# Attention score products over 128 rows, query loads per tile, and norm sums in groups of 128 tokens

## The chip, the cores and the metric

The kernel runs on one core of a Trainium2 chip. The time is the device time of one execution, in microseconds (us). The engines are named as in the profile: PE is TensorE (PEld its weight loads), DVE is VectorE, ACT is ScalarE, POOL is GpSimd, and SP is SyncE, which only issues DMAs. POOL and SP each execute their queue in order, DMA issues included.

## What is computed

One step of a backbone of two layers over 128 prompt tokens and 512 latent tokens (a grid of 8 x 64), model width 1024. A layer normalises its input, runs four mixers A to D side by side, merges them, and ends with a feed-forward part. The change touches the norm, the scores of B (differential attention, 4 heads of two 64-wide maps) and those of D (neighbourhood attention, 8 heads of width 64):

```python
def _rmsnorm(x, g):
    y = xf * lax.rsqrt(jnp.mean(xf * xf, axis=-1, keepdims=True) + EPS)
...
def _diff_attend(q, k, v, lam):            # B
    p = jax.nn.softmax(jnp.einsum('bhqmd,bhkmd->bhmqk', qi, k).astype(F32) * scale, axis=-1)
    pd = p[:, :, 0] - lam * p[:, :, 1]
    return jnp.einsum('bhqk,bhkd->bhqd', pd, v.astype(F32)).astype(q.dtype)
...
def _na_latent(q, k, v, ck, cv, rpb):      # D, latent queries; 16-column window as a mask
    s_lat = jnp.einsum('bhqd,bhkd->bhqk', qi, ki).astype(F32) * scale + bias
    s_ctx = jnp.einsum('bhqd,bhkd->bhqk', qi.astype(F32), ckf) * scale
    p = jax.nn.softmax(jnp.concatenate([s_ctx, s_lat], axis=-1), axis=-1)
```

Prompt queries read the prompt's own keys alone; latent queries read 256 cached context keys and the latent keys.

## The kernel before

**Exact products from two parts.** Every large product is made of float32r operands split into a high and a low part (`split`: ACT copies the high part, DVE subtracts). A weight tile is loaded by SP into a raw buffer (`load_w`; two raw buffers), ACT casts it to `whi`, DVE makes 608 columns of the rest `wlo` and POOL the last 416. `unit` (line 292) then issues three products of 320 columns for each of eight feature tiles: high by high, low by high, high by low, all over 128 rows. One weight tile so feeds 48 products. In the profile they are `pu`, the "stream" of the text; `ptk` are products of the same kind with 256 columns.

**Who sets the order.** `weave` writes the order of PE by hand. The mixers are chains (Python generators) with ranks; a chain yields the tiles that its next PE work waits for, a rough clock says when they are there, and until then steps of the projections, gates and merges (`fill`) are issued. That clock charges a score product by its columns alone. DVE, ACT, POOL and SP get their order from a scheduler with priorities, and tiles of one pool are handed out as they come free. The pool `sa` has 18 tiles of 128 x 512 (`NSA`), shared by all chains. B and D both wait for branch A to be done, and then run side by side, with the stream between their steps.

**Scores of B** (`mix_b`, `b_tile`). `prep_b` leaves each head's turned queries and keys in DRAM (`bqk`), as blocks of 64 rows: high 0, low 0, low 1, high 1. `mix_b` loads for a head, on POOL's queue (`QM`): `qd`, for each of two maps the high part of all 512 queries twice, one copy under the other (64 + 64 rows); `ql`, both maps' low parts (128 rows, one map in each half); and `Kd`, per map the keys' high part over their low part. `split_ctx` makes the same of the 256 context keys (`Kc`). For one query tile of 128 and one map, `latent` then issues, for 512 latent keys and again for 256 context keys, two products into one bank: `qd` over 128 rows gives high by (high + low), `ql` over 64 rows adds low by high. Maximum, exponent, sum, turning and the product with the values follow in `b_tile`. The prompt tile is one product of 64 rows in plain float32 for either map.

**Scores of D** (`mix_d`). The same with head pairs in place of maps: `qd`, `ql`, `kd`, `kc`, loaded by SP (`QD`) from `dqk`. Queries come in four blocks of 16 columns (128 queries); a block reads 256 context keys and a window of 8 x 24 or 8 x 32 latent keys (`WIN`), so eight products: two heads, two key pieces, high and low. Line 1426 yields what they wait for.

**Norm** (`rstd_half`; for the first input, `first`). Squares of 320 tokens are summed over features by products with one column of ones, 64 tokens at a time; a chain of small DVE instructions (`rsqrt`) makes the factor; DVE spreads it on a diagonal (`dg`, 64 rows of 320), and a product with ones over 64 rows, `prs`, copies it to all partitions.

## Time and profile before

| what | value |
|---|---|
| median of 3 runs | 3595.67 us (3592.9 to 3596.69) |
| profiled execution, span from first to last instruction | 3582.7 us |
| PE busy | 3465.2 us, 97% |
| weight loads (PEld) busy | 3312.7 us, 92% |
| DVE busy | 2366.4 us, 66% |
| ACT busy | 1430.6 us, 40% |
| POOL busy | 511.7 us, 14% |

The span is 13.0 us under the median; what lies around it (start and end of the execution) is in no row. Shares of busy time are averages over stages that differ. Ends of products on PE are modelled and overlap, so the distance from one start to the next is what tells the cost of a product. The mixers of layer 0 fill the time to some 1200 us, merging and feed-forward that to some 1850, and layer 1 follows the same way.

### The profile page before, as it was taken

The numbers are of one execution on the slowest core, as the hardware profiler recorded it, in microseconds if no ns is written. First come the engines' busy times: TensorE is split into PE (matmuls) and PEld (weight loads), VectorE is DVE, ScalarE is ACT, GpSimd is POOL, SyncE is SP. The second block draws the span as 40 slices with busy tenths as digits, with TensorE's granted clock in tenths as the row PEclk, the third lists the DMA queues.
The fourth block names the chain that finished last, engine by engine and source line by source line (L and its number), as shares of the span: only waits on it lengthen the run. The fifth ranks groups of instructions, "written<-read, shape, count | busy, mean of one in ns | idle before, by whom it ended". The sixth has DMA issues, their size and how long they took to land.

```text
span 3582.7 us, 63638 instructions
## 1 busy us (share of the span) xinstructions
PE 3465.2 (97%) x24036; PEld 3312.7 (92%) x24036; DVE 2366.4 (66%) x5487; ACT 1430.6 (40%) x3170; POOL 511.7 (14%) x536
## 2 busy tenths in 40 slices
PE   8999999899999999999999999998999999999998
PEld 5988999888989999999999999998888999999998
DVE  7689888865566478787456897776444546634445
ACT  5344545444343253222253454554444433522222
POOL 2221112311112100000002212223121121000000
PEclk9999999999999999999999999999999999999999
DMA  6443434854243254444234433356343134312222
GB/s 217 152 151 129 128 109 135 250 155 144 94 139 110 96 172 143 150 150 131 82 120 140 143 120 105 104 158 205 112 138 120 59 99 146 115 63 77 80 77 71
DMA packets 282826, 455.96 MB, mean 127 GB/s; under 512 B 46996, under 2 KB 175636, under 8 KB 282520
## 3 DMA queue, kind: packets, MB, share of 16 engines
q1 hardware_dynamic: 272472, 421.48, 36.9%
q0 software_dynamic: 10048, 30.42, 2.8%
q8 instruction: 190, 3.11, 0.4%
q14 instruction: 116, 0.95, 0.1%
HBM read 364.23 MB, written 87.56 MB: 126 GB/s over the span
## 4 chain that ended last, share of the span: by engine, by line
PE 72%; DVE 6%; DMA 4%; issue 3%; ACT 2%; POOL 0%; SPq 0%; DVEq 0%; ACTq 0%; POOLq 0%
PE pu L150 53%; PE ptk L150 2%; PE pbs L150 2%; PE pds L150 2%; PE pdv L150 2%; PE pbo L150 1%; PE pW L150 1%; PE pX L150 1%; PE pca L150 1%; PE pdt L156 1%; PE pT L150 1%; DMA wraw<-in_wd 1%; PE pkS L150 1%; DVE wlo L105 1%; DMA moT<-oT 0%
## 5 line engine op out<-in xcount | busy, mean ns | idle before, releaser
L150 PE MATMUL pu<-hh,whi 128*128 128x320 f32 (+1 forms) x3760 | 1199.9, 320 | 18.3 <-ACT stg L105 15.7
L150 PE MATMUL pu<-hl,whi 128*128 128x320 f32 (+1 forms) x3760 | 1168.0, 311 | 2.9 <-DVE hl L105 2.9
L150 PE MATMUL pu<-hh,wlo 128*128 128x320 f32 (+1 forms) x3760 | 1168.5, 311 | 0.0
L150 PEld LDWEIGHTS pu<-hh,whi 128*128 128x128 f32 (+1 forms) x3760 | 710.6, 189 | 29.5 <-ACT stg L105 16.4
L150 PEld LDWEIGHTS pu<-hl,whi 128*128 128x128 f32 (+1 forms) x3760 | 710.8, 189 | 4.7 <-DVE hl L105 3.1
L150 PEld LDWEIGHTS pu<-hh,wlo 128*128 128x128 f32 (+1 forms) x3760 | 709.0, 189 | 1.7
L105 ACT CAST whi<-wraw 128x1024 fp32r<-128x1024 f32 (+2 forms) x410 | 390.7, 953 | 680.8 <-PE pu L150 441.3
L105 POOL TENSOR_TENSOR wlo<-wraw,whi 128x416 fp32r<-128x416 f32 (+1 forms) x209 | 320.5, 1534 | 1886.3 <-ACT whi L105 1409.2
L105 DVE TENSOR_TENSOR wlo<-wraw,whi 128x608 fp32r<-128x608 f32 (+3 forms) x410 | 385.6, 940 | 282.6 <-ACT whi L105 274.0
L150 PE MATMUL pu<-fa,whi 128*128 128x320 f32 x1152 | 253.7, 309 | 0.2 <-DVE x L105 0.2
L150 PE MATMUL pu<-mo,whi 128*128 128x320 f32 x1024 | 235.4, 317 | 5.4 <-DVE mo L105 3.4
L105 DVE SCALAR_TENSOR_TENSOR x<-pu,gn,x 128x128 f32<-128x128 f32 (+1 forms) x336 | 136.5, 435 | 88.1 <-PE pu L150 86.2
L150 PEld LDWEIGHTS pu<-fa,whi 128*128 128x128 f32 x1152 | 192.7, 188 | 0.5 <-PE pu L150 0.5
L150 PE MATMUL ptk<-whi,hh 128*128 128x256 f32 x640 | 192.5, 301 | 0.0
L150 PE MATMUL ptk<-wlo,hh 128*128 128x256 f32 x640 | 182.6, 285 | 3.2 <-DVE wlo L105 3.2
L150 PE MATMUL ptk<-whi,hl 128*128 128x256 f32 x640 | 182.5, 285 | 0.0
L491 DVE CUSTOM_DVE_ANT_0 junk<-wa,cs,mod 128x256 bf16<-128x256 f32 (+1 forms) x288 | 172.2, 598 | 14.6 <-DMA wa<-in_wada 10.5
L150 PEld LDWEIGHTS pu<-mo,whi 128*128 128x128 f32 x1024 | 171.8, 190 | 9.8 <-DVE mo L105 4.9
L150 PE MATMUL pu<-fa,wlo 128*128 128x320 f32 x576 | 177.8, 309 | 0.0
L150 PE MATMUL pu<-mo,wlo 128*128 128x320 f32 x512 | 159.6, 312 | 0.0
L150 PEld LDWEIGHTS ptk<-wlo,hh 128*128 128x128 f32 x640 | 124.0, 194 | 3.4 <-DVE wlo L105 3.4
L150 PEld LDWEIGHTS ptk<-whi,hh 128*128 128x128 f32 x640 | 124.2, 194 | 0.0
(426 smaller groups left out, 6170.1 us busy)
## 6 DMA issues: line engine op xcount, KB each, us to landing
wraw<-in_win SPq DMA_DIRECT2D x151, 512.0 KB, 3.8
wa<-in_wada SPq DMA_DIRECT2D x116, 256.0 KB, 2.9
wraw<-in_wg SPq DMA_DIRECT2D x44, 512.0 KB, 3.6
wraw<-in_wu SPq DMA_DIRECT2D x44, 512.0 KB, 3.6
wraw<-in_wd SPq DMA_DIRECT2D x80, 256.0 KB, 2.6
p<-stg SPq DMA_DIRECT2D x112, 160.0 KB, 3.3
wa<-in_wada SPq DMA_DIRECT2D x128, 128.0 KB, 2.5
wraw<-in_wtok SPq DMA_DIRECT2D x32, 512.0 KB, 4.0
```

What stands on the lines that cost most here:

```text
L105: r = f(*args, **kw)
L150: r = self.nc.tensor.matmul(out, lhsT, rhs, start=start, stop=stop)
L156: r = self.nc.tensor.transpose(out, src, ident)
L491: self.nc.vector.tensor_tensor_reduce(junk, raw, cs[g], 0.5, o if k0 else self.bada[:, l, m:m + 1], ALU.mult, ALU.add, o)
```

## The change

Four things are edited; comments go too.

- **Score products over 128 rows.** For every query tile a tile `bqt` or `dqt` of 128 x 512 holds four blocks of 128 columns: for B high 0, low 0, low 1, high 1, for D high and low of either head, each stacked twice (64 + 64 rows). High and low products both read 128 rows, and both use the whole stacked key tile.
- **Queries loaded per tile.** `queries` loads that tile with two DMAs of 64 rows by four runs of 128 columns; the tile of t+1 is asked for before tile t is worked on. The loads of `qd` and `ql` are gone.
- **Prompt products padded.** POOL clears a tile `bpr` or `dpr` of 256 columns, two DMAs put the two heads' (maps') keys on its diagonal blocks, and one product over 128 rows and 256 columns gives both heads' scores, in one bank in place of two.
- **Norm sums by 128 tokens.** Three groups that start at tokens 0, 128 and 192 (the last two overlap); the diagonal is built by `spread` in two DVE instructions over 128 rows.

```diff
+TOK = (0, 128, 192)
...
-        for t in range(5):
+        for t, o in enumerate(TOK):
             for i, s_ in enumerate((acc, sq)):
-                self.mm(ps[:64, t:t + 1], s_[:, t * 64:t * 64 + 64], self.ones[:, 0:1], start=i == 0, stop=i == 1)
-        ms = self.sm("ms", 5)[:64]
-        v.tensor_scalar(ms, ps[:64, :5], 1.0 / D, EPS, ALU.mult, ALU.add)
-        r = self.rsqrt(ms, 5, "rms")
-        dg = self.GS("dg", HT)[:64]
-        v.tensor_tensor(dg.rearrange("p (t c) -> p t c", t=5), bc1(self.ident[:64, :64], 5), bc(r, 64), ALU.mult)
+                self.mm(ps[:, t:t + 1], s_[:, o:o + 128], self.ones[:, 0:1], start=i == 0, stop=i == 1)
+        ms = self.sm("ms", 3)
+        v.tensor_scalar(ms, ps[:, :3], 1.0 / D, EPS, ALU.mult, ALU.add)
+        dg = self.spread(self.rsqrt(ms, 3, "rms"))
         pb = self.M("prs")
-        self.mm(pb[:, :HT], self.ones[:64, :], dg, start=True, stop=True)
+        self.mm(pb[:, :HT], self.ones, dg, start=True, stop=True)
         return pb
 
+    def spread(self, r):
+        dg = self.GS("dg", HT)
+        self.v.tensor_tensor(dg[:, :256].rearrange("p (t c) -> p t c", t=2), bc1(self.ident, 2), bc(r[:, :2], 128), ALU.mult)
+        self.v.tensor_scalar(dg[:, 256:], self.ident[:, 64:], r[:, 2:3], None, ALU.mult)
+        return dg
...
-            for t in range(10):
-                self.mm(ps[:64, t:t + 1], accs[t // 5][:, t % 5 * 64:t % 5 * 64 + 64], self.ones[:, 0:1], start=True, stop=True)
-            ms = self.sm("ms1", 10)[:64]
-            v.tensor_scalar(ms, ps[:64, :10], 1.0 / D, EPS, ALU.mult, ALU.add)
-            r = self.rsqrt(ms, 10, "rm1")
-            dgs = []
-            for j in range(2):
-                dg = self.GS("dg")[:64]
-                v.tensor_tensor(dg.rearrange("p (t c) -> p t c", t=5), bc1(self.ident[:64, :64], 5), bc(r[:, j * 5:j * 5 + 5], 64), ALU.mult)
-                dgs.append(dg)
+            for t in range(6):
+                self.mm(ps[:, t:t + 1], accs[t // 3][:, TOK[t % 3]:TOK[t % 3] + 128], self.ones[:, 0:1], start=True, stop=True)
+            ms = self.sm("ms1", 6)
+            v.tensor_scalar(ms, ps[:, :6], 1.0 / D, EPS, ALU.mult, ALU.add)
+            r = self.rsqrt(ms, 6, "rm1")
+            dgs = [self.spread(r[:, j * 3:j * 3 + 3]) for j in range(2)]
...
         yield wait
+        if nb == 1:
+            both = self.M("pbs")
+            score(both[:, :256])
         for m in range(2):
             if m and nb > 1:
                 yield es[0],
             pss = []
             for i, w in enumerate(ws):
+                if nb == 1:
+                    pss.append(both[:, m * 128:m * 128 + 128])
+                    continue
                 ps = self.M("pbs")[:, :w]
                 score(ps, m, i)
...
-            cx = self.SA("bcx")
-            cv, qp, kp = cx[:, :256], cx[:, 256:384], cx[:, 384:512]
-            self.dma(cx[:, 256:].rearrange("p (i c) -> p i c", i=2), self.pd['qk', h][:, :, :128].rearrange("i p c -> p i c"), QM)
+            cx, pr = self.SA("bcx", 384), self.SA("bpr", 256)
+            cv, qp = cx[:, :256], cx[:, 256:384]
+            self.g.memset(pr, 0.0)
+            for m in range(2):
+                self.dma(pr[m * 64:m * 64 + 64, m * 128:m * 128 + 128], self.pd['qk', h][1, m * 64:m * 64 + 64, :128], QM)
+            self.dma(qp, self.pd['qk', h][0, :, :128], QM)
             self.dma(cv, self.I['cvb'][l, h], QM)
-            qd, Kd = [self.SA("bqd", dt=F32R) for _ in range(2)], [self.SA("bKd", dt=F32R) for _ in range(2)]
-            ql, Kc = self.SA("bql", dt=F32R), self.SA("bKc", dt=F32R)
+            Kd, Kc = [self.SA("bKd", dt=F32R) for _ in range(2)], self.SA("bKc", dt=F32R)
             Kc = [Kc[:, 0:256], Kc[:, 256:512]]
             dq, dk = self.bqk[h][0], self.bqk[h][1]
+            def queries(t):
+                x = self.SA("bqt", dt=F32R)
+                src = dq[:, t * 128 - 128:t * 128].rearrange("(b p) c -> p b c", b=4)
+                for i in range(2):
+                    self.dma(x[i * 64:i * 64 + 64].bitcast(F32).rearrange("p (b c) -> p b c", b=4), src, QM)
+                return x
+            qt = {1: queries(1)}
             for m in range(2):
-                for i in range(2):
-                    self.dma(qd[m][i * 64:i * 64 + 64].bitcast(F32), dq[192 * m:192 * m + 64], QM)
                 self.dma(Kd[m].bitcast(F32), dk[128 * m:128 * m + 128], QM)
-            self.dma(ql.bitcast(F32), dq[64:192], QM)
             o = self.S("bo")
             self.split_ctx(Kc, o, self.I['ckb'][l, h])
             fin = self.sm("b_f", 5)
 
-            def prompt(ps, m, i):
-                r_ = slice(m * 64, m * 64 + 64)
-                self.mm(ps, qp[r_, :], kp[r_, :], start=True, stop=True)
+            def prompt(ps):
+                self.mm(ps, qp, pr, start=True, stop=True)
 
             for t in range(5):
                 c, cl = slice(t * 128, t * 128 + 128), slice(t * 128 - 128, t * 128)
 
                 def latent(ps, m, i):
-                    r_, K = slice(m * 64, m * 64 + 64), (Kd, Kc)[i][m]
-                    self.mm(ps, qd[m][:, cl], K, start=True, stop=False)
-                    self.mm(ps, ql[r_, cl], K[r_, :], start=False, stop=True)
+                    K, x = (Kd, Kc)[i][m], qt[t]
+                    hi, lo = 3 * m, 1 + m
+                    self.mm(ps, x[:, hi * 128:hi * 128 + 128], K, start=True, stop=False)
+                    self.mm(ps, x[:, lo * 128:lo * 128 + 128], K, start=False, stop=True)
+                if 0 < t < 4:
+                    qt[t + 1] = queries(t + 1)
                 if t:
                     vs = [vt[:, j * 128:j * 128 + 128] for j in range(1, 5)] + [cv[:, 0:128], cv[:, 128:256]]
-                    yield from self.b_tile(latent, (512, 256), vs, neglam, o[:, c], fin[:, t:t + 1], (qd[1], Kd[1], ql, Kc[1]))
+                    yield from self.b_tile(latent, (512, 256), vs, neglam, o[:, c], fin[:, t:t + 1], (qt[t], Kd[1], Kc[1]))
...
-            cx = self.SA("dcx")
-            cv, q, k = cx[:, 0:256], cx[:, 256:384], cx[:, 384:512]
+            cx, pr = self.SA("dcx", 384), self.SA("dpr", 256)
+            cv, q = cx[:, 0:256], cx[:, 256:384]
+            self.g.memset(pr, 0.0)
+            for hh in range(2):
+                self.dma(pr[hh * 64:hh * 64 + 64, hh * 128:hh * 128 + 128], self.pd[48 + hp][hh * 64:hh * 64 + 64, :128], QD)
+            self.dma(q, self.pd[44 + hp][:, :128], QD)
             self.dma(cv, self.I['cvd'][l, hp], QD)
-            self.dma(q, self.pd[44 + hp][:, :128], QD)
-            self.dma(k, self.pd[48 + hp][:, :128], QD)
-            qd, kd = [self.SA("dqd", dt=F32R) for _ in range(2)], [self.SA("dkd", dt=F32R) for _ in range(2)]
-            ql, kc = self.SA("dql", dt=F32R), self.SA("dkc", dt=F32R)
+            kd, kc = [self.SA("dkd", dt=F32R) for _ in range(2)], self.SA("dkc", dt=F32R)
             kc = [kc[:, 0:256], kc[:, 256:512]]
             od = self.S("dod")
             dq, dk = self.dqk[hp][0], self.dqk[hp][1]
+            def queries(b):
+                x = self.SA("dqt", dt=F32R)
+                src = dq[:, :, b * 128:b * 128 + 128].rearrange("i (h p) c -> p (i h) c", h=2)
+                for i in range(2):
+                    self.dma(x[i * 64:i * 64 + 64].bitcast(F32).rearrange("p (b c) -> p b c", b=4), src, QD)
+                return x
+            qt = {0: queries(0)}
             for hh in range(2):
-                r_ = slice(hh * 64, hh * 64 + 64)
                 for i in range(2):
-                    p_ = slice(i * 64, i * 64 + 64)
-                    self.dma(qd[hh][p_].bitcast(F32), dq[0, r_], QD)
-                    self.dma(kd[hh][p_].bitcast(F32), dk[i ^ hh, r_], QD)
-            self.dma(ql.bitcast(F32), dq[1], QD)
+                    self.dma(kd[hh][i * 64:i * 64 + 64].bitcast(F32), dk[i ^ hh, hh * 64:hh * 64 + 64], QD)
             self.split_ctx(kc, od, self.I['ckd'][l, hp])
-            yield q, k, vf
+            yield q, pr, vf
             pv = self.M("pdv")
             self.tp(pv[:, :128], vf[:, :128], self.ident)
             vp = self.Q("dvp")
             a.copy(vp, pv[:, :128])
             o = self.Q("do")
-            pss = [self.M("pds"), self.M("pds")]
+            ps = self.M("pds")
             P = self.SA("dP")
             P, PT = P[:, :256], P[:, 256:]
             rcs = []
+            self.mm(ps[:, :256], q, pr, start=True, stop=True)
             for hh in range(2):
-                r_ = slice(hh * 64, hh * 64 + 64)
-                self.mm(pss[hh][:, :128], q[r_, :128], k[r_, :128], start=True, stop=True)
-            for hh in range(2):
+                c = slice(hh * 128, hh * 128 + 128)
                 nm, ss, rc = self.sm("d_nm", 1), self.sm("d_ss", 1), self.sm("d_rc", 1)
-                v.tensor_reduce(nm, pss[hh][:, :128], AX.X, ALU.max, negate=True)
-                a.activation(P[:, hh * 128:hh * 128 + 128], pss[hh][:, :128], ACT.Exp, bias=nm, accum_out=ss)
+                v.tensor_reduce(nm, ps[:, c], AX.X, ALU.max, negate=True)
+                a.activation(P[:, c], ps[:, c], ACT.Exp, bias=nm, accum_out=ss)
                 v.reciprocal(rc, ss)
                 rcs.append(rc)
             yield P,
             for hh in range(2):
-                self.tp(pss[0][:, 256 + hh * 128:384 + hh * 128], P[:, hh * 128:hh * 128 + 128], self.ident)
-            a.copy(PT, pss[0][:, 256:512])
+                self.tp(ps[:, 256 + hh * 128:384 + hh * 128], P[:, hh * 128:hh * 128 + 128], self.ident)
+            a.copy(PT, ps[:, 256:512])
...
-                yield bias, qd[1], kd[1], ql, kc[1]
+                if b < 3:
+                    qt[b + 1] = queries(b + 1)
+                yield bias, qt[b], kd[1], kc[1]
                 Ps, rcs = [], []
                 pss = []
                 for hh in range(2):
-                    r_ = slice(hh * 64, hh * 64 + 64)
                     ps = self.M("pds")
-                    qa, la = qd[hh][:, b * 128:b * 128 + 128], ql[r_, b * 128:b * 128 + 128]
+                    qa, la = (qt[b][:, i * 128:i * 128 + 128] for i in (hh, 2 + hh))
                     ka = kd[hh].rearrange("p (r c) -> p r c", c=64)[:, :, k0:k0 + wc]
                     for o_, x in ((ps[:, :256], kc[hh]), (ps[:, 256:256 + nk], ka)):
                         self.mm(o_, qa, x, start=True, stop=False)
-                        self.mm(o_, la, x[r_], start=False, stop=True)
+                        self.mm(o_, la, x, start=False, stop=True)
                     pss.append(ps)
```

PE's order, in layer 0 where a map of B stands ahead of a block of D (`pbs` are B's scores, `pds` D's, `pu` the stream, `pdv` the turning of D's values). Before:

```order
L150 MATMUL pbo<-bv,be 128x128
L150 MATMUL pbs<-bKd,bqd 128x512
L150 MATMUL pbs<-bKd,bql 128x512
L150 MATMUL pbs<-bKc,bqd 128x256
L150 MATMUL pbs<-bKc,bql 128x256
L150 MATMUL pu<-hh,whi 128x320
L150 MATMUL pu<-hl,whi 128x320
L150 MATMUL pu<-hh,wlo 128x320
L150 MATMUL pds<-dkc,dqd 128x256
L150 MATMUL pds<-dkc,dql 128x256
```

Now:

```order
L152 MATMUL pbo<-bv,be 128x128
L152 MATMUL pbs<-bKd,bqt 128x512 x2
L152 MATMUL pbs<-bKc,bqt 128x256 x2
L152 MATMUL pu<-hh,whi 128x320
L152 MATMUL pu<-hl,whi 128x320
L152 MATMUL pu<-hh,wlo 128x320
L152 MATMUL pds<-dkc,dqt 128x256 x2
L152 MATMUL pds<-dkd,dqt 128x256 x2
L152 MATMUL pds<-dkc,dqt 128x256 x2
```

Before, the list ends with the first two of a block's eight products, now with six. Only the score rows differ: each pair reads one query tile, and the stream stands between B and D as it did.

POOL's queue at the first head of B in layer 0 (`wlo` are the weights' low parts, `rr` and `bqk` belong to `prep_b`). Before:

```order
L161 DMA bcx<-qk_94 128x2x128
L161 DMA bcx<-in_cvb 128x256
L161 DMA bqd<-bqk_102 64x512 x2
L161 DMA bKd<-bqk_102 128x512
L161 DMA bqd<-bqk_102 64x512 x2
L161 DMA bKd<-bqk_102 128x512
L161 DMA bql<-bqk_102 128x512
L161 DMA rr<-qk_96 32x2x512
L105 TENSOR_TENSOR wlo<-wraw,whi 128x416
L161 DMA rr<-qk_96 32x2x512
```

Now:

```order
L107 MEMSET bpr 128x256
L163 DMA bcx<-qk_94 128x128
L163 DMA bpr<-qk_94 64x128 x2
L163 DMA bcx<-in_cvb 128x256
L163 DMA bqt<-bqk_102 64x4x128 x2
L163 DMA bKd<-bqk_102 128x512 x2
L107 MEMSET dpr 128x256
L163 DMA rr<-qk_96 32x2x512 x2
L107 TENSOR_TENSOR wlo<-wraw,whi 128x416 x3
```

Two memsets and the padded keys came in, the query loads of the whole head became those of one tile. The next tiles' loads stand later on the same queue, between pieces of weights:

```order
L163 DMA bqt<-bqk_102 64x4x128 x2
L107 TENSOR_TENSOR wlo<-wraw,whi 128x416 x4
L163 DMA bqt<-bqk_102 64x4x128 x2
L107 TENSOR_TENSOR wlo<-wraw,whi 128x416
L163 DMA bqt<-bqk_102 64x4x128
L107 MEMSET dpr 128x256
```

What moved there are the query loads alone; the weight pieces keep their order behind one another.

## Rows read from the trace of the kernel before

**Rows 1.** The page: busy time by engine, and the chain that ended last, by line.

```profile
PE 3465.2 (97%) x24036; PEld 3312.7 (92%) x24036; DVE 2366.4 (66%) x5487; ACT 1430.6 (40%) x3170; POOL 511.7 (14%) x536
...
PE pu L150 53%; PE ptk L150 2%; PE pbs L150 2%; PE pds L150 2%; PE pdv L150 2%; PE pbo L150 1%; PE pW L150 1%; PE pX L150 1%; PE pca L150 1%; PE pdt L156 1%; PE pT L150 1%; DMA wraw<-in_wd 1%; PE pkS L150 1%; DVE wlo L105 1%; DMA moT<-oT 0%
```

**Rows 2.** Stretches: us, busy PE, PEld, DVE, ACT, POOL (instructions), granted clock, DMA, GB/s.

```profile
0.00:700.00 700.00, 644.29 (x4697) 606.06 (x4697) 575.77 (x1310) 329.49 (x725) 156.70 (x186) 0.98 0.49 157
700.00:1160.00 460.00, 455.37 (x2970) 414.42 (x2971) 283.72 (x886) 198.11 (x537) 83.95 (x81) 0.99 0.43 133
...
1900.00:2450.00 550.00, 525.38 (x4040) 515.59 (x4039) 437.12 (x844) 268.35 (x585) 134.19 (x152) 0.98 0.43 134
2450.00:2970.00 520.00, 509.68 (x3295) 465.20 (x3295) 255.24 (x709) 212.76 (x569) 98.51 (x89) 0.98 0.36 112
...
3200.00:3300.00 100.00, 100.00 (x684) 100.00 (x683) 40.64 (x74) 22.87 (x38) 0.00 (x0) 1.00 0.23 71
```

**Rows 3.** Timeline of PE, layer 0, one map of B: start us, busy us, what.

```profile
743.31 0.47 PE L150 MATMUL pbs<-bKd,bqd 128*128 128x512 f32 x1
743.71 0.49 PE L150 MATMUL pbs<-bKd,bql 64*128 64x512 f32 x1
744.13 0.38 PE L150 MATMUL pbs<-bKc,bqd 128*128 128x256 f32 x1
...
744.76 0.41 PE L150 MATMUL pu<-hh,whi 128*128 128x320 f32 x1
745.01 0.31 PE L150 MATMUL pu<-hl,whi 128*128 128x320 f32 x1
```

**Rows 4.** Timeline of PE, two blocks of D: first product, first instruction after the eighth.

```profile
722.35 0.28 PE L150 MATMUL pds<-dkc,dqd 128*128 128x256 f32 x1
...
724.62 0.42 PE L156 MATMUL pdv<-cst,dvw 128*96 128x128 f32 x2
...
745.30 0.28 PE L150 MATMUL pds<-dkc,dqd 128*128 128x256 f32 x1
...
747.70 0.44 PE L156 MATMUL pdv<-cst,dvw 128*128 128x128 f32 x2
```

**Rows 5.** Timeline of PE, layer 1, products of 256 columns over 128 rows.

```profile
2151.75 0.28 PE L150 MATMUL ptk<-whi,hl 128*128 128x256 f32 x1
...
2154.38 0.28 PE L150 MATMUL ptk<-whi,hh 128*128 128x256 f32 x1
```

**Rows 6.** Instructions of tiles pbs and pds: count, ns min/median/max, first and last start, forms.

```profile
L150 PE MATMUL pbs<-bKd,bqd x64: 387/474/502, 743.3 to 2963.3; 128*128 128x512 f32 x64
...
L150 PE MATMUL pds<-dkd,dqd x64: 354/372/582, 722.9 to 2852.9; 128*128 128x192 f32 x32, 128*128 128x256 f32 x32
```

**Rows 7.** Timeline of the weight loads (PEld) in the place of rows 3.

```profile
744.13 0.19 PEld L150 LDWEIGHTS pbs<-bKc,bqd 128*128 128x128 f32 x1 [0.24 <-issue]
```

**Rows 8.** Timeline of PE, prompt products of B, layer 0.

```profile
706.00 0.49 PE L150 MATMUL pbs<-bcx 64*128 64x128 f32 x4
706.42 0.41 PE L150 MATMUL pu<-hh,whi 128*128 128x320 f32 x1
706.67 0.31 PE L150 MATMUL pu<-hl,whi 128*128 128x320 f32 x1
```

**Rows 9.** Timeline of PE, spreading product of the last norm.

```profile
3557.58 0.80 PE L150 MATMUL prs<-dg,cst 64*128 64x320 f32 x2
3558.31 0.42 PE L150 MATMUL pu<-fa,spl 128*128 128x320 f32 x1
```

**Rows 10.** Groups of POOL (count, busy, mean ns, idle before); waits of the SP queue.

```profile
L161 POOL DMA_DIRECT2D bqd<-bqk x32 | 16.9, 531 | 2.7 <-DMA rx<-qk 2.0 <-DMA rr<-qk 0.7
...
L161 POOL DMA_DIRECT2D bcx<-qk x8 | 5.9, 735 | 0.0
...
SPq L281 <- DVE wlo L105: 1207.3, 342, 20.5
```

**Rows 11.** Groups of ACT, 700 to 1200 us: busy, mean ns, idle before, releasers.

```profile
L105 ACT CAST whi<-wraw 128x1024 fp32r<-128x1024 f32 x44 | 46.2, 1050 | 49.7 <-PE pu L150 28.8 <-issue 19.9 <-DMA wraw<-in_wbr 0.9
```

More of the change, by code (lines that the diff above doesn't have):

```diff
@@ L618, in first @@
             pb = self.G1("prs")
-            self.mm(pb[:, :HT], self.ones[:64, :], dg, start=True, stop=True)
+            self.mm(pb[:, :HT], self.ones, dg, start=True, stop=True)
             pbs.append(pb)
@@ L1183, in latent @@
                 def latent(ps, m, i):
-                    r_, K = slice(m * 64, m * 64 + 64), (Kd, Kc)[i][m]
-                    self.mm(ps, qd[m][:, cl], K, start=True, stop=False)
-                    self.mm(ps, ql[r_, cl], K[r_, :], start=False, stop=True)
+                    K, x = (Kd, Kc)[i][m], qt[t]
[4 more added lines that the diff above has]
+                    qt[t + 1] = queries(t + 1)
                 if t:
                     vs = [vt[:, j * 128:j * 128 + 128] for j in range(1, 5)] + [cv[:, 0:128], cv[:, 128:256]]
-                    yield from self.b_tile(latent, (512, 256), vs, neglam, o[:, c], fin[:, t:t + 1], (qd[1], Kd[1], ql, Kc[1]))
+                    yield from self.b_tile(latent, (512, 256), vs, neglam, o[:, c], fin[:, t:t + 1], (qt[t], Kd[1], Kc[1]))
                 else:
-                    yield from self.b_tile(prompt, (128,), [vt[:, :128]], neglam, o[:, c], fin[:, t:t + 1], (qp, kp))
+                    yield from self.b_tile(prompt, (128,), [vt[:, :128]], neglam, o[:, c], fin[:, t:t + 1], (qp, pr))
             ms = self.sm("bms", 5)
```

## The prediction

> **What bounds the kernel now.** I read the page first. Of a span of 3582.7 us TensorE (PE) is busy for 3465.2 us, 97%, and the next working engine, VectorE (DVE), for 66% [rows 1]. That alone proves little, since matmul ends are modelled, so I looked at what ended last: the chain of waits runs through PE's products, the projections `pu` with 53% of the span, and `pbs` and `pds`, the score products of branches B and D, with 2% each [rows 1]. Then the table by stretches: B and D run from about 700 to 1160 us (layer 0) and 2450 to 2970 us (layer 1), 980 us in all, and PE idles there for only 4.6 and 10.3 us; in the stretches that hold branches A and C it idles for 55.7 of 700 us and 24.6 of 550 us, with DVE at 82% and 79% against 62% and 49% in B and D [rows 2]. So where the change acts PE is the bound, and time taken out of PE's row comes out of the end unless something else turns late. The granted clock is 0.98 to 0.99 there, the 2.4 GHz level [rows 2].
>
> The last view is PE's own timeline, and the numbers to read in it are the starts. A busy span of 0.38 us says nothing, because matmuls overlap; the distance to the next start is what a product costs. For 320 columns, the projections, it is 100/684 = 0.146 us, from a stretch that holds nothing else [rows 2]; for 256 columns it is 0.1195 us: 2151.75 to 2154.38, 22 products later [rows 5]. The score products stand out. High part over 128 rows, low part over 64 rows, and back: 743.31, 743.71, 744.13, and 744.76 two products on, so 0.40 and 0.42 us for 512 columns and 0.63 for two of 256, and the stream product after them takes 0.25 instead of 0.146 [rows 3]. Whatever the column count, about 0.2 us is added wherever the row count changes, and the weight load at such a place starts together with its product, at 744.13 after 0.24 us of idle load path, instead of ahead of it [rows 7].
>
> **Score products of B.** After the change hi and lo stand over 128 rows, so I price them like other products over 128 rows with a new weight each. The slope between 256 and 320 columns is (0.146 - 0.1195)/64, some 0.41 ns a column, which gives 0.226 us for 512. Four products and the stream product behind them then take 2 x 0.226 + 2 x 0.120 + 0.146 = 0.84 us, where they now take 745.01 - 743.31 = 1.70 us [rows 3]. That is 0.86 us for one map of one query tile, and there are 64 [rows 6]: **55.0 us**. The columns are not fewer: the low part now multiplies the key's low part too, at no column more.
>
> **Score products of D.** A block of 16 query columns with a 256-column window takes 747.70 - 745.30 = 2.40 us for eight products; at 0.120 us each they take 0.96: 1.44 us saved. With the 192-column window it is 724.62 - 722.35 = 2.27 us [rows 4]. For 192 columns I have no undisturbed row: the slope says 0.093 us, the next wider row 0.120; I take the middle, 0.107, so 0.91 us for the block and 1.36 us saved. There are 16 blocks of either kind (64 window products of the high part, two heads of 32 blocks, half of them 192 wide) [rows 6]: 23.0 + 21.8 = **44.8 us**.
>
> **Prompt products.** Now two small products on different halves of the rows run together: four passes from 706.00 to 706.42, and the stream product behind them ends its turn at 706.67, 0.10 us late [rows 8]. Padded with zeros they become one product of twice the columns. It may cost 0.21 us (half of today's, if the passes merge) up to 0.58 (256/320 of the 0.73 us that the two 320-column passes of `prs` take, switches included [rows 9]); I take 0.42, the row nearest in kind. Then the 0.10 us behind it goes, and as much ahead of it: 0.2 us in each of 16 places, 3.2 us, with bounds of 0.6 and 6.6.
>
> **Norm sums.** One norm of a half has ten tiny sums over 64 tokens and one spreading product over 64 rows in two passes, 0.73 us [rows 9]. Now there are six sums over 128 tokens and a spread over 128 rows: two switches of some 0.2 us less on PE, against one more small DVE instruction where the spread matrix is built, in a serial chain. Were it as dear as the switches are, nothing would be left; if it is hidden, 0.4 us goes. For ten spreads, most beside other products, I take 2 us of gain, bounds 4 and, if the DVE instruction shows twice over, -3. The gain so far: 55.0 + 44.8 + 3.2 + 2 = **105 us** of PE's row.
>
> **Loads and memsets.** Per head of B, GpSimd (POOL) issues eight loads of a quarter each instead of five, now in 512-byte runs; the load with as many runs costs POOL 0.73 us, a plain one 0.53 [rows 10]. Per head that is some 8 x 0.73 + 6 x 0.53 against 0.73 + 8 x 0.53, and two memsets, one for B and one for D, which I take at an issue's 0.53 us each: about 5 us more, 41 us for eight heads. POOL is busy for 84 of 460 us there [rows 2], so the time itself is hidden; what it can hold up are the pieces `wlo` of the weights that queue behind on POOL. On SyncE (SP) a head of D issues 12 DMAs now and 16 then; the weight loads behind them wait, but SP itself spends 1207 us waiting for DVE to free a raw weight tile [rows 10], which covers 4 more issues. Both at nothing; the price if the cover goes is the third rival. Each query load is issued one tile ahead, and the PE order, row by row, is the old one with only the score, prompt and norm rows replaced, so no product moves.
>
> **What is late next.** With 105 us out of 980 the same DVE work stands in 878 us: 283.7/410 is 69%, 255.2/468 is 55%, together 61% after 55%. PE idles 1.5% of these 980 us at a DVE share of 55%, and 6.4% of the two stretches of A and C at 81% [rows 2]. Along that line 6 points bring 1.2% of 878 us, **11 us**, of new waiting; bounds zero (the fills between a chain's steps were inserted with no cost for the switches) and 55 us (the 8.0% of the first stretch). Net 105 - 11 = 94 us.
>
> **Against the span.** All this is made on the profiled execution, 3582.7 us of span. The median is 3595.67, so 13.0 us lie outside the span and stay: 3595.67 - 94 = **3502 us**.
>
> **Rivals.** *Waits take half back.* The chains of B and D (scores, maximum, exponent, turning, products) lose cover; PE comes to each step sooner and waits for DVE or ScalarE. For: the steps of a chain are serial, and the switches now fall inside them. Against: only 4.6 us of idle time stand in the first stretch and 10.3 in the second [rows 2]. At the 8.0% of the first stretch the waits are 70 us instead of 15: 3595.67 - 105 + 55 = 3546 us.
>
> *Weight loads come into the open.* Now a load at a switch waits for it anyway; afterwards hi and lo use the same rows throughout. If a load could not run beside a product over the same rows, each of the 512 products would add its load, 0.19 us [rows 7], 97 us, and 3588 us is left. Against: the products of `ptk` also use all rows with a new weight each and start 0.1195 us apart, less than one load lasts [rows 5], so loads do run beside them. The Trainium skill, "TensorE: Matmul & The Clock Gate", Part 3, says that a weight load overlaps matmuls in flight only where the row group differs; by that sentence this rival would hold. The trace disagrees, as the row of `ptk` shows, so it gets a small chance.
>
> *POOL's queue starves PE, and the kernel is slower.* Each pair of query loads needs a free tile of the shared pool of 18; POOL executes in order, so while it waits for PE or a landing, the weight pieces `wlo` behind it stand, and then PE. There are 32 pairs; to eat 105 us each must hold PE by 3.3 us, and at 5 us each the time is 3595.67 - 105 + 160 = 3651 us. For: POOL's queue does mix loads and weight pieces. Against: a weight tile feeds 48 products, 7 us of PE, and ScalarE, ahead of converting 44 weight tiles there, waits 28.8 us for PE, so weights are made ahead [rows 11].
>
> **How the numbers follow.** Forecast case (80 to 114 us gained) 0.78, waits take half back 0.15, loads in the open 0.03, POOL's queue 0.04. The range reaches from 3482 (111 us with the upper bounds of prompts and norms and 0.093 us for 192 columns, no new waits, and some 3 us of today's gone) to 3546, the first rival; both ends hold about 0.87. A measurement of this kernel can tell some 0.2%, 7 us, from no change: faster 0.93, same 0.03, slower 0.04.
>
> **What would show it.** Right: `pbs` and `pds` products over 128 rows starting 0.23 and 0.12 us apart, no weight load with idle time before it between them, the stream product behind them at 0.146 us; B's and D's stretches near 413 and 472 us; PE idle there 1.5 to 4%. Wrong: distances still at 0.3 us, PE waiting for `wlo` of POOL or for `dPl` and `be`, or the stretches shortened while others grow.

## The result, and the profile after

The changed kernel takes **3500.48 us** (median of four runs, 3495.77 to 3503.89), the kernel before 3594.91 us (four runs, 3592.9 to 3596.69) beside it: a ratio of 0.9738, 95% interval 0.9719 to 0.9756, or 94 us less (88 to 101). The forecast was 3502 us. The profiled execution took 3495.77 us with a span of 3493.8 us, so 2.0 us lie outside the span.

The page of the changed kernel, busy time by engine (beside rows 1):

```profile
PE 3366.3 (96%) x23932; PEld 3294.3 (94%) x23932; DVE 2366.3 (68%) x5497; ACT 1427.7 (41%) x3170; POOL 544.1 (16%) x592
```

PE is still the bound, with 99 us less of busy time for the same result. DVE does the same work in less time; POOL has 32.4 us more, the loads in quarters and memsets.

The stretches from the first to the last score product of a layer (columns as in rows 2), of the kernel before:

```profile
706.00:1196.30 490.30, 485.67 (x3174) 441.83 (x3174) 296.50 (x918) 206.96 (x558) 89.67 (x82) 0.99 0.41 126
2471.70:2964.80 493.10, 482.78 (x3103) 438.48 (x3103) 243.21 (x690) 201.05 (x543) 87.58 (x75) 0.98 0.34 107
```

and of the changed one:

```profile
700.90:1155.00 454.10, 440.16 (x3162) 434.14 (x3161) 295.73 (x918) 206.34 (x559) 101.06 (x109) 0.98 0.48 142
...
2432.00:2875.00 443.00, 428.99 (x3090) 422.91 (x3090) 234.89 (x679) 197.16 (x538) 100.26 (x99) 1.00 0.43 126
```

The two stretches shrink from 983.4 to 897.1 us, 86.3 of the 88.9 us by which the spans differ: the gain lies where the score products stand. Stretch less busy time is PE's idle time: 4.6 and 10.3 us before, 13.9 and 14.0 after, so **13.0 us of new idle time**. PE's busy time there falls from 968.5 to 869.2 us.

One map of B behind a stream product. Before, timeline of PE (start us, busy us, what):

```profile
756.30 0.40 PE L150 MATMUL pbs<-bKd,bqd 128*128 128x512 f32 x1
756.63 0.50 PE L150 MATMUL pbs<-bKd,bql 64*128 64x512 f32 x1
757.06 0.39 PE L150 MATMUL pbs<-bKc,bqd 128*128 128x256 f32 x1
757.38 0.38 PE L150 MATMUL pbs<-bKc,bql 64*128 64x256 f32 x1
757.68 0.41 PE L150 MATMUL pu<-hh,whi 128*128 128x320 f32 x1
757.94 0.31 PE L150 MATMUL pu<-hl,whi 128*128 128x320 f32 x1
```

The same map after (x2 in a row: two products of the same name, merged; the start is the first one's), and the weight load of its first product (timeline of PEld):

```profile
754.04 0.63 PE L152 MATMUL pbs<-bKd,bqt 128*128 128x512 f32 x2
754.51 0.40 PE L152 MATMUL pbs<-bKc,bqt 128*128 128x256 f32 x2
754.75 0.31 PE L152 MATMUL pu<-hh,whi 128*128 128x320 f32 x1
754.90 0.31 PE L152 MATMUL pu<-hl,whi 128*128 128x320 f32 x1
```

```profile
753.90 0.34 PEld L152 LDWEIGHTS pbs<-bKd,bqt 128*128 128x128 f32 x2
```

Two products of 512 columns take 0.47 us and two of 256 columns 0.24, so 0.235 and 0.12 each; the stream product behind them takes 0.15 instead of 0.26. The load of the first product begins at 753.90, 0.14 us ahead of it, while the stream product that started at 753.89 runs; in rows 7 the load of a product behind a change of rows began together with that product. The map takes 0.86 us where it took 1.64.

### The profile page after: what moved, and what is told of

Same layout as the page of the kernel before. It is cut to its first block, busy times and chain, and to the rows that moved or that the text cites. A ratio compares the mean times of both kernels' runs of the same rounds, so it can differ in the third digit from the quotient of the medians.

```text
span 3493.8 us, 63676 instructions
## 1 busy us (share of the span) xinstructions
PE 3366.3 (96%) x23932; PEld 3294.3 (94%) x23932; DVE 2366.3 (68%) x5497; ACT 1427.7 (41%) x3170; POOL 544.1 (16%) x592
## 4 chain that ended last, share of the span: by engine, by line
PE 69%; DVE 6%; DMA 5%; issue 3%; ACT 2%; POOL 1%; SPq 0%; DVEq 0%; ACTq 0%; POOLq 0%
PE pu L152 54%; PE ptk L152 2%; PE pdv L152 1%; PE pbs L152 1%; PE pbo L152 1%; PE pW L152 1%; PE pX L152 1%; PE pdt L158 1%; PE pT L152 1%; PE pca L152 1%; PE pds L152 1%; DVE cacc L107 1%; DMA wraw<-in_wd 1%; DVE wlo L107 1%; DMA moT<-oT 1%
## 5 line engine op out<-in xcount | busy, mean ns | idle before, releaser
L152 PE MATMUL pu<-hh,whi 128*128 128x320 f32 (+1 forms) x3760 | 1195.8, 318 | 18.1 <-ACT stg L107 14.9
L152 PEld LDWEIGHTS pu<-hh,whi 128*128 128x128 f32 (+1 forms) x3760 | 709.2, 189 | 22.6 <-ACT stg L107 15.4
L498 DVE CUSTOM_DVE_ANT_0 junk<-wa,cs,mod 128x256 bf16<-128x256 f32 (+1 forms) x288 | 171.7, 596 | 24.9 <-DMA wa<-in_wada 20.8
```

The costliest lines, as they stand in the source:

```text
L152: r = self.nc.tensor.matmul(out, lhsT, rhs, start=start, stop=stop)
L498: self.nc.vector.tensor_tensor_reduce(junk, raw, cs[g], 0.5, o if k0 else self.bada[:, l, m:m + 1], ALU.mult, ALU.add, o)
```

## The experiments

Each edit is shown against the kernel that its text names. Runs of one kernel scatter, and the scatter goes with the mean granted clock of TensorE: the kernel before, run beside the first experiments, took from 3582.91 us at 0.986 to 3603.05 us at 0.982. A ratio to the kernel before on the same chip is good to some 0.2% either way, 7 us. A difference between two changed kernels is therefore good to some 9 us (estimated from two such intervals), and a smaller step is not told from none.

**Low products of B and D on 64 rows again.**

```diff
-                    self.mm(ps, x[:, lo * 128:lo * 128 + 128], K, start=False, stop=True)
+                    self.mm(ps, x[r_, lo * 128:lo * 128 + 128], K[r_], start=False, stop=True)
...
-                        self.mm(o_, la, x, start=False, stop=True)
+                        self.mm(o_, la[r_], x[r_], start=False, stop=True)
```

> The changed kernel, but with the low score products of B and D on the 64 rows of their own half again; query loads per tile, padded prompt products and norm sums in 128-token groups stay. Theory (the changes of row count between score products cost PE 55 us in B and 46 in D, and some 11 to 13 us of that came back as waits): the time goes from 3500 back to about 3590 (3583 to 3596), the rest of the change keeping some 5 us; products after a change of rows start 0.4 us apart again. Rival (the gain comes from loading the queries per tile, with less in flight at a head's start): stays near 3500. Rival (prompt and norm edits carry much of it): 3560 to 3580.

Measured: 3589.34 us, ratio 0.9992 (0.9977 to 1.0007). With all other edits in place nothing measurable is left of the gain. Loads per tile, prompts and norms come to 3 us together (from 8 us gained to 3 lost), not told from zero; a small gain by prompts and norms and a small loss by the loads can stand in it side by side. The stretches of the run:

```profile
704.20:1201.00 496.80, 485.84 (x3159) 443.39 (x3158) 298.83 (x919) 207.67 (x559) 103.35 (x109) 0.99 0.44 130
2479.50:2967.50 488.00, 479.76 (x3090) 436.89 (x3089) 240.03 (x680) 198.47 (x538) 99.64 (x99) 0.99 0.39 114
```

PE idles 11.0 and 8.2 us there, 19.2 in all. So of the 13.0 us of new idle time 4.3 come with the other edits, and 8.7 with the row change.

**Low products of B alone on 64 rows again** (the first of the two edits above).

> The changed kernel, with the low score products of B alone on 64 rows again (64 maps of four products). Theory: 55 us of PE's row come back, less some 6 us of waits that go: 3549 (3542 to 3556), all of it in the stretches of B and D; D's products stay 0.12 and 0.09 us apart. Rival (loads per tile): 3500. Rival (waits have taken back much of B's gain, since a map's scores stand in a serial chain): 3515 to 3535.

Measured: 3546.14 us, ratio 0.9879 (0.985 to 0.9908): 46 us above the changed kernel by the medians, 51 by the ratios. B is worth about half of the gain; D, by the step from here to the run above, 43 us. No large part of B's gain is eaten by its serial chain, and the rival of the loads per tile is out.

**The kernel before, with B's low parts duplicated and loaded for the whole head.**

```diff
-            ql, Kc = self.SA("bql", dt=F32R), self.SA("bKc", dt=F32R)
+            ql, Kc = [self.SA("bql", dt=F32R) for _ in range(2)], self.SA("bKc", dt=F32R)
...
-            self.dma(ql.bitcast(F32), dq[64:192], QM)
+            for m in range(2):
+                for i in range(2):
+                    self.dma(ql[m][i * 64:i * 64 + 64].bitcast(F32), dq[64 + 64 * m:128 + 64 * m], QM)
...
-                    self.mm(ps, ql[r_, cl], K[r_, :], start=False, stop=True)
+                    self.mm(ps, ql[m][:, cl], K, start=False, stop=True)
```

> The kernel before, with one edit: B's low parts of the queries stand in two tiles, each duplicated over both halves of the rows, loaded for the whole head at once like the high parts, and B's low products go over 128 rows. D, prompts and norms are as before. Theory: 55 us of PE's row go, less some 6 us of new waits: 3595 - 49 = 3546 (3540 to 3553). Rival (it is the loads per tile that bring it): 3595, or slower by the two loads more per head.

Measured: 3545.84 us, ratio 0.9875 (0.9852 to 0.9899), 45 us less (36 to 53). The gain of B comes without loads per tile. The same edit for B and D together needs more tiles than the pool of 18 has; it wasn't tried.

**The kernel before, with half of B's row changes.**

```diff
                     self.mm(ps, qd[m][:, cl], K, start=True, stop=False)
-                    self.mm(ps, ql[r_, cl], K[r_, :], start=False, stop=True)
+                    if i == 0:
+                        first[0] = ps
+                    else:
+                        self.mm(first[0], ql[r_, cl], Kd[m][r_, :], start=False, stop=True)
+                        self.mm(ps, ql[r_, cl], K[r_, :], start=False, stop=True)
```

> The kernel before, with one edit: the four score products of a map of B are issued high, high, low, low instead of high, low, high, low; all rows, tiles and loads as before. Two changes of row count per map instead of four. Theory (each change there and back costs 0.43 us): 64 x 0.43 = 27 us less, 3568 (3562 to 3574), the two high products 0.23 and 0.12 us apart. Rival (a product over 64 rows is slow in itself, or its low operand's load is): 3595, since there are as many of them. Rival (loads per tile): 3595.

Measured: 3567.95 us, ratio 0.9929 (0.9904 to 0.9955). Timeline of PE in one map, the one of rows 3:

```profile
743.65 0.48 PE L150 MATMUL pbs<-bKd,bqd 128*128 128x512 f32 x1
743.97 0.28 PE L150 MATMUL pbs<-bKc,bqd 128*128 128x256 f32 x1
744.17 0.49 PE L150 MATMUL pbs<-bKd,bql 64*128 64x512 f32 x1
744.51 0.28 PE L150 MATMUL pbs<-bKc,bql 64*128 64x256 f32 x1
744.72 0.42 PE L150 MATMUL pu<-hh,whi 128*128 128x320 f32 x1
744.97 0.31 PE L150 MATMUL pu<-hl,whi 128*128 128x320 f32 x1
```

The same four products, the same rows and loads, take 1.32 us to the second stream product instead of 1.70 [rows 3]. 64 times 0.38 is 24 us; measured are 24 us by the medians and 26 by the ratio (16 to 34). What costs is the change of the row count, not the product over 64 rows: there are as many of those as before. The price lies on both sides of a change: the 256-column product ahead of one takes 0.20 instead of 0.12, the 512-column one behind it 0.34 instead of 0.235. The Trainium skill, "TensorEngine Tiling (Array Packing)", Key Properties, says that changing the tiling mode drains TensorE. These rows fit it with some 0.2 us lost at a change; that what passes in this time is a drain, no row shows.

**Where the new waits come from.** The longest wait in the changed kernel, on PE, then DVE, then SP's queue:

```profile
860.50 1.12 PE L158 MATMUL pdt<-cst,dPl 128*128 128x128 f32 x4 [6.86 <-ACT dPl L107]
```

```profile
858.60 0.49 DVE L107 CUSTOM_DVE_ANT_0 pds<-pds,dbias,d_mc 128x256 f32<-128x256 f32 x1 [5.57 <-DMA dbias<-in_nab]
```

```profile
849.70 0.43 SPq L163 DMA_DIRECT2D dbias<-in_nab  x1
850.17 1.29 SPq L163 DMA_DIRECT2D dqt<-dqk  x2
```

PE waits 6.86 us for ACT's exponents `dPl`, ACT for DVE, and DVE for a load: the bias of D's block, issued at 849.70, when the score products to which it is added have already started (849.11). The last name in PE's wait is not the cause. The kernel's rough clock counts 2.3 us (`DLAT`) for a load; the landing of `dbias` in the kernel before, then in the changed one, then in the run with B's and D's low products on 64 rows:

```profile
DMA to landing us min/median/max: 2.4/3.6/7.9
```

```profile
DMA to landing us min/median/max: 3.1/4.7/8.9
```

```profile
DMA to landing us min/median/max: 2.7/4.6/10.2
```

PE's waits for `dPl` over the whole execution (us in total, times, longest), in the same order:

```profile
PE pdt L156 <- ACT dPl L105: 6.4, 2, 4.6
```

```profile
PE pdt L158 <- ACT dPl L107: 15.4, 5, 6.9
```

```profile
PE pdt L158 <- ACT dPl L107: 11.0, 3, 6.8
```

So, in one execution each, the bias lands later with 64 rows too, and the longest wait is nearly as long there. Of the 9.0 us by which these waits grow, 4.6 come with the other edits and 4.4 with the row change. Which of the other edits makes the bias land later was not tested apart; the query loads per tile are the nearest.

The wait costs more than itself. PE stands idle from 853.64 to 860.50, and the window that begins in it (columns as in rows 2) reads:

```profile
856.00:866.00 10.00, 5.50 (x22) 5.50 (x23) 3.39 (x14) 3.90 (x9) 1.67 (x1) 0.50 0.68 162
```

The granted clock is 1.00 from 850 to 856 us, and then 0.50, the 1.2 GHz level, to 866; the stream products behind the wait start 0.27 us apart instead of 0.146. From 850 to 856 us, with the bias on its way, the DMA engines are busy for 96% of the time; that this is why it lands so late was not tested.

**Query loads twice.**

```diff
-                for i in range(2):
+                for i in (0, 1, 0, 1):
                     self.dma(x[i * 64:i * 64 + 64].bitcast(F32).rearrange("p (b c) -> p b c", b=4), src, QM)
...
-                for i in range(2):
+                for i in (0, 1, 0, 1):
                     self.dma(x[i * 64:i * 64 + 64].bitcast(F32).rearrange("p (b c) -> p b c", b=4), src, QD)
```

> The changed kernel, with each query load of a tile issued twice, into the same tile: 64 more loads on GpSimd's queue for B, 64 more on SyncE's queue for D. Theory as predicted (queries are there a tile ahead and the queues have room, so the loads cost nothing): 3500 (3496 to 3505). Rival (the query loads stand in SyncE's queue ahead of D's bias, whose late landing makes PE wait 6.86 us for dPl at 860.50 in the changed kernel): each doubled load delays it by 0.65 us, and the waits for dPl rise from 15 us by 5 to 15: 3506 to 3515.

Measured: 3515.9 us, ratio 0.9787 (0.9766 to 0.9809), 15 us more. The loads are not free under this doubling, and the waits for `dPl` rise as the rival said, to 24.9 us. But the experiment is cruder than meant: the second load writes the tile of the first, and waits on its queue until that has landed. Who waited for `bqt` in this run (us, times):

```profile
  POOL bqt L163: 75.7, 30
```

On SP's queue the waits for `dqt` are 81.9 us in 31. So the run prices queues held up by waits, not loads alone. To part the queues, the edit for B alone:

> The changed kernel, with the query loads of B alone issued twice into the same tile, on GpSimd's queue. The second load also waits there until the first has landed (75.7 us in 30 waits in the run with both branches' loads doubled), so that GpSimd's queue is held up some 2.5 us per tile. Theory (the 15 us that the doubled loads of both branches cost lie on SyncE's queue, ahead of D's bias): 3500 (3496 to 3505). Rival (GpSimd's queue holds up wlo and then PE): 3508 to 3516.

Measured: 3505.7 us, ratio 0.9752 (0.9734 to 0.9771), 5 us more, not told from none, and between the two forecasts. Holding POOL's queue for 2.5 us per tile costs little or nothing; the other 10 us, just outside the scatter, came when D's loads on SP were doubled as well.

**D's query loads on POOL's queue.**

```diff
-                    self.dma(x[i * 64:i * 64 + 64].bitcast(F32).rearrange("p (b c) -> p b c", b=4), src, QD)
+                    self.dma(x[i * 64:i * 64 + 64].bitcast(F32).rearrange("p (b c) -> p b c", b=4), src, QM)
```

> The changed kernel, with the query loads of D issued on GpSimd's queue, as those of B are, instead of SyncE's; none is doubled. Theory (D's bias lands late partly because two query loads of 0.65 us each stand ahead of the next bias on SyncE's queue, and share its transfers): VectorE's 7.5 us of waits for dbias shrink below 4, and the time is 3494 (3490 to 3498). Rival (the bias is late for its tile of the pool or for the weights transferred at the same time, whatever queue the queries are on): 3500 (3497 to 3505), VectorE's waits for dbias as before.

Measured: 3507.9 us, ratio 0.9782 (0.9757 to 0.9807). The theory missed: the time went up, by 7 us by the medians and 16 by the ratios, and DVE waits as long for the bias as before. Its waits (us, times) in the changed kernel, and then in this run:

```profile
  DMA dbias<-in_nab: 7.5, 3
```

```profile
  DMA dbias<-in_nab: 7.2, 2
```

It is not the query loads ahead of it on SP's queue that make the bias late. POOL's queue stands idle for 14.2 us in four waits for PE ahead of D's query loads; whether that makes this run slower than the changed kernel is open.

**The bias one block ahead.** `window(b)` is the old load of a block's bias.

```diff
             self.split_ctx(kc, od, self.I['ckd'][l, hp])
+            bt = {0: window(0)}
...
-                bias = self.SA("dbias").rearrange("p (h k) -> p h k", h=2)[:, :, :nk]
-                self.dma(bias, self.I['nab'][l, 2 * hp:2 * hp + 2, :, BOFF[b]:BOFF[b] + nk].rearrange("h p k -> p h k"))
                 if b < 3:
+                    bt[b + 1] = window(b + 1)
                     qt[b + 1] = queries(b + 1)
+                bias = bt[b]
```

> The changed kernel, with D's bias loaded one block ahead (the first block's before the prompt products), as the queries are, instead of at the block that uses it. Theory (PE's 15 us of waits for dPl in the changed kernel are partly waits for the bias: VectorE stands 7.5 us in three places until it lands): VectorE's waits for dbias go, PE's waits for dPl fall below 8 us, and the time is 3493 (3488 to 3498). Rival (another operand of the same step is as late, or the pool of 18 tiles, which now holds one more, delays other loads): 3500 or more.

Measured: **3484.0 us** (3476.93 to 3487.58), ratio 0.9694 (0.9676 to 0.9712): faster than both kernels, and by more than expected. Its stretches, PE's waits for `dPl` over the whole execution, and the page's first row:

```profile
699.40:1147.70 448.30, 440.82 (x3189) 434.29 (x3188) 301.37 (x924) 205.50 (x560) 103.18 (x110) 1.00 0.49 145
2423.70:2846.40 422.70, 416.30 (x3019) 411.16 (x3018) 229.76 (x672) 195.74 (x536) 97.94 (x98) 1.00 0.44 128
```

```profile
PE pdt L158 <- ACT dPl L107: 4.2, 3, 3.0
```

```profile
PE 3360.4 (97%) x23932; PEld 3288.7 (95%) x23932; DVE 2367.7 (68%) x5497; ACT 1426.2 (41%) x3170; POOL 543.6 (16%) x592
```

DVE waits for the bias no longer, PE's waits for `dPl` fall from 15.4 to 4.2 us, and its idle time in the stretches from 27.9 to 13.9, below the 14.9 of the kernel before. Of the 18.6 us by which the spans of the two profiled executions differ, 12.7 are idle time of PE; the other 5.9 are busy time, for the same 23932 products. The clock fits that: the granted clock of the two stretches is 1.00 and 1.00 here, 0.98 and 1.00 in the changed kernel.

**The same early bias without the row change, and in the kernel before** (the edits above, combined).

> The version with D's bias loaded one block ahead, with the low score products of B and D on 64 rows again. Theory (with the bias early, the change of rows gives its whole PE time and nothing back): by the product starts of the two traces B's maps take 49.9 us less and D's blocks 46.1 us, so 3484 + 96 = 3580 (3575 to 3585). Rival (what the quicker products give back does not hang on the bias): the difference stays near the 89 us that it is without the early bias, 3573 or less.

Measured: 3579.48 us, ratio 0.9953 (0.9937 to 0.9969), 95.5 us above the version with all rows. By the ratios it is 93 us, and 91 without the early bias, so the times alone don't part the two theories. The idle time in the stretches, of one execution each, leans to the first:

```profile
701.60:1201.00 499.40, 493.86 (x3188) 451.53 (x3187) 306.13 (x926) 209.23 (x561) 103.86 (x110) 0.99 0.44 130
2472.10:2950.00 477.90, 471.96 (x3018) 429.77 (x3017) 235.96 (x679) 198.63 (x541) 99.67 (x101) 0.98 0.38 114
```

PE idles 11.5 us here and 13.9 with all rows: 2.4 us given back where with the late bias it was 8.7. Over the whole executions the two figures are 1.7 and 3.7 us, so this is a hint and no proof.

> The kernel before, with one edit: D's bias loaded one block ahead. Theory (the late bias is mostly laid open by the change: in the kernel before PE waits 6.4 us for dPl in two places, in the changed one 15.4 us in five): 3594 - 6 = 3588 (3583 to 3592). Rival (the late bias costs the kernel before as much as the changed one, and has nothing to do with the change): 16 us less, 3577.

Measured: a ratio of 0.9983 (0.9972 to 0.9995), so 6 us less (2 to 10) than the kernel before, as the theory said; the rival's 16 us are out. In the changed kernel the early bias brings 16 us by the ratios (7 to 25). So the bias was a little late already, and after the change its lateness is probably dearer: the two intervals just touch. As shown above, the row change is only part of that.

**More or less slack** (one number; the second run on the version with the early bias).

```diff
-SLACK = 220.0
+SLACK = 350.0
```

> The changed kernel, with SLACK, the margin by which a chain's next products are issued after their operands are estimated to be there, raised from 220 to 350 ns. Rival to the theory of late loads (score products are now as quick as the rough clock of the kernel says, so that PE comes to every step of a chain a little early, and a little more margin helps everywhere): the 13 us of new idle time shrink by half, 3494 (3489 to 3498). Theory (a few long waits, for loads that land late or at a head's start, which 0.13 us doesn't cover): 3500 (3496 to 3505).

> The version with D's bias loaded one block ahead, with SLACK 120 instead of 220 ns. The run with 350 ns was 16 us slower than the changed kernel, its idle time of PE lying elsewhere. Theory (SLACK acts by the places to which it moves the steps of the chains, and not by the margin itself): no forecast of a sign, 3484 with 10 us either way. Rival (a smaller margin is better, as 350 was worse): 3470 to 3478.

Measured: 3516.28 us (ratio 0.979, 0.9771 to 0.981), 16 us more than with 220; and with 120 ns 3530.69 us (0.9826, 0.9809 to 0.9842), 47 us more than 3484. Both are slower, and neither theory gave the time: the forecasts were 3500 and 3494, and 3484 with 10 us either way and 3470 to 3478. The stretch of layer 1 with 350 ns:

```profile
2401.00:2903.00 502.00, 479.32 (x3418) 473.03 (x3419) 282.36 (x743) 224.56 (x590) 130.04 (x139) 0.98 0.46 134
```

It holds 3418 instructions of PE instead of 3090, and 22.7 us idle instead of 14.0: the chains have moved against the stream. The waits for `dPl` fall there too, to 1.9 us, and the run is slower all the same. So neither run says what a margin does by itself.

## Why the prediction was right, and where it was off

**The mechanism held.** Putting the low products back on 64 rows takes back the whole gain, taking out half of B's row changes brings half of B's gain, and B's edit alone, on the kernel before, brings the whole of it.

**B's score products: 55.0 us, measured 49 to 50.** The slope was right (0.235 and 0.12 us where 0.226 and 0.120 were taken). The step that was off is to price every map by rows 3 against products in the stream. That map stands behind `pbo`, a chain product; there the first product also takes longer after the change:

```profile
743.28 0.71 PE L152 MATMUL pbs<-bKd,bqt 128*128 128x512 f32 x2
743.83 0.40 PE L152 MATMUL pbs<-bKc,bqt 128*128 128x256 f32 x2
744.07 0.31 PE L152 MATMUL pu<-hh,whi 128*128 128x320 f32 x1
744.21 0.31 PE L152 MATMUL pu<-hl,whi 128*128 128x320 f32 x1
```

It takes 0.55 us for the first two instead of 0.47, so 0.93 for the map (to 744.21) against 1.70: 0.77 us saved. Behind a stream product it is 1.64 to 0.86: 0.78. Not 0.86 in either place; 64 times 0.77 to 0.78 is 49 to 50.

**D's: 44.8 us, measured about 45 by two blocks.** A block with 192 and one with 256 columns, first product and first instruction behind the eighth:

```profile
718.32 0.40 PE L152 MATMUL pds<-dkc,dqt 128*128 128x256 f32 x2
...
719.22 0.38 PE L158 MATMUL pdv<-cst,dvw 128*96 128x128 f32 x2
```

```profile
744.51 0.40 PE L152 MATMUL pds<-dkc,dqt 128*128 128x256 f32 x2
...
745.47 0.38 PE L158 MATMUL pdv<-cst,dvw 128*128 128x128 f32 x2
```

0.90 and 0.96 us, where 0.91 and 0.96 were forecast, against 2.27 and 2.40 [rows 4]: 16 x 1.37 + 16 x 1.44.

**Prompts: 3.2 us, measured 3 by one place. Norms: 2 us, measured some 2 by one spread.** A prompt product, and the spread of a norm:

```profile
700.90 0.59 PE L152 MATMUL pbs<-bpr,bcx 128*128 128x256 f32 x2
701.15 0.49 PE L152 MATMUL pu<-hh,whi 128*128 128x320 f32 x1
701.48 0.31 PE L152 MATMUL pu<-hl,whi 128*128 128x320 f32 x1
```

```profile
1271.78 0.80 PE L152 MATMUL prs<-dg,cst 128*128 128x320 f32 x2
1272.18 0.55 PE L152 MATMUL pu<-mgh,whi 128*128 128x320 f32 x1
1272.56 0.31 PE L152 MATMUL pu<-mgl,whi 128*128 128x320 f32 x1
```

The padded product takes 0.25 us, not the 0.42 that was taken, but the stream product behind it takes 0.33, more than two of its kind elsewhere; why is not shown (the padded product is in plain float32, two passes). Together 0.58 against 0.67 [rows 8], and 0.1 us ahead of it (the stream product there takes 0.15 instead of 0.24): about the forecast, by two errors that cancel. The spread takes 0.40 instead of 0.73 [rows 9], but 0.38 goes to the product behind it instead of 0.25 (as behind the change of rows in rows 3), so 0.2 us is saved, ten times. The totals don't show it: outside the two stretches PE is busy for 2496.8 us before and 2497.1 after.

**New waits: 11 us, measured 13.0 of idle time; the reason was another, so the near hit is luck.** The forecast drew a line between DVE's share and PE's idle time, for chains that lose cover. DVE's share did go to 59%, but the waits are no broad loss: the longest are few, at heads' and blocks' beginnings, and a late load stands behind the longest. The step that failed is "Loads and memsets", which took the loads for hidden at nothing: it misses the bias, which the prediction doesn't name. An early bias takes 14 us of the idle time away again, and 4.3 of the 13.0 us are there without the row change. POOL's share was near what was said (41 us forecast, 32.4 measured, as a memset takes 0.32 us and not 0.53, and a query load 0.62 and not 0.73), and hidden.

**The sum.** 49.5 + 45 + 3 + 2 is some 100 us, less 13.0 us of new idle time is 87; the spans differ by 88.9 (over the whole executions 98.9 us less busy time and 10.0 more idle time). The forecast had 105 - 11 = 94.

**Of the 13.0 us outside the span, 2.0 are real.** That step is wrong: 2.0 us lie outside in the changed kernel, and the runs of the kernel before beside the experiments have spans some 1.8 us short of their times (3590.4 for 3592.23). By that, an estimate, the profiled execution of the kernel before took some 3585 us, 10 less than its median; its runs beside the experiments lie between 3582.91 and 3603.05. The forecast, worked out as a difference to the median, doesn't suffer from it, but its hit to 2 us is partly luck: against the profiled execution, 3582.7 - 94 = 3489 misses the span of 3493.8 by 5.

**The rivals.** Waits took back 13 of 100 us, not half. Weight loads did not come into the open: they start ahead of their products, and products over the same rows with new weights start 0.12 us apart while a load takes 0.19. The Trainium skill's sentence in "TensorE: Matmul & The Clock Gate", Part 3, on row groups, taken by itself, doesn't hold for these products. POOL's queue did not starve PE: with B's loads doubled, and 78.9 us of waits for their landing put into that queue, the time rose by 5 us, not told from none.

## What to carry to other kernels

Where small products of 64 and 128 rows take turns, fill the smaller up to 128 rows (here the duplicated rows cost PE no time), or at least group them by row count: each change cost some 0.2 us, nearly as much as a product of 512 columns. When PE gets quicker, follow its longest new waits back through ACT and DVE to the load behind them, and move that load one step ahead; a wait that ends can give back clock as well as its own length. Where a rough clock sets the order by hand, judge its margins by the time of the whole, since with either change here the run was slower.

## What the runs showed of the hardware

- A change between 64 and 128 rows costs some 0.2 us, split between the product ahead of it and the one behind it (0.08 and 0.10 us in the map with two changes).
- A product of 512 columns behind a chain product of 128 columns in plain float32 (`pbo`) takes 0.31 us (0.55 for two, less 0.235), 0.08 more than behind a stream product, with no change of rows; and the stream product behind a two-pass float32 product of 256 or 320 columns takes 0.33 to 0.38 us instead of 0.146.
- The granted clock fell to the 1.2 GHz level within a wait of PE of 6.86 us and stood there for the 10 us from 856 to 866; stream products then started 0.27 us apart. In the two stretches with the early bias, where PE's longest wait is 3.1 us, it reads 1.00.
